# SiLU as one ScalarE activation in a hybrid DeltaNet/GLA layer: `Silu` in place of `Tanh` and a VectorE product

## The chip, the cores and the metric

The kernel runs on one core of a Trainium2 chip. That core has TensorE (PE in the profile; its weight loads are shown apart as PEld), VectorE (DVE), ScalarE (ACT), GpSimd (POOL) and SyncE (SP, which here only issues transfers). Each engine works through its own instruction list in order and waits on semaphores for what other engines have to deliver. The metric is the device time of one launch in microseconds (us), as the median of several runs. Beside it stands one profiled execution, whose trace gives every instruction's start and length.

## The reference: what is computed

One transformer layer on 1024 tokens of width 1024, in fp32. SiLU, x·sigmoid(x), occurs in three places:

```python
qkv = jax.nn.silu(causal_depthwise_conv(jnp.concatenate([gq, gk_, gv], -1), gdn_conv_w[i]))
q_a = l2norm(to_chunks(cq, GDN_HEADS)) * (GDN_HEAD_DIM ** -0.5)
k_a = l2norm(to_chunks(ck, GDN_HEADS))
o_a = gated_delta_rule_chunked(q_a, k_a, v_a, g, beta)
o_a = rmsnorm(o_a, gdn_norm_g[i]) * jax.nn.silu(gz)        # DeltaNet output gate
...
o_b = rmsnorm(gla_chunked(q_b, k_b, v_b, log_fg), gla_norm_g[i]) * jax.nn.silu(lr)   # GLA output gate
merged = jax.nn.sigmoid(gate_a) * y_a + jax.nn.sigmoid(gate_b) * y_b
x = x + merged @ w_out[i]
x = x + CrossAttn(rmsnorm(x), rmsnorm(mem))                # softmax over 256 memory tokens
x = x + relu(rmsnorm(x) @ w1)**2 @ w2                      # then a final rmsnorm
```

The branch A heads (8 of them, gated DeltaNet) need a triangular inverse per chunk and a scan over chunks; the branch B heads (4, gated linear attention, GLA) need exponentials of cumulated gates and a scan.

## The kernel before, in words

Activations are kept transposed: 128 channels on the partitions, tokens along the free axis in two halves of 512. All large products ("dense" products below) are done in three passes: an fp32 operand is split into a rounded high part and the remainder, `split` (L575 to L578): ScalarE copies the high part (L577), VectorE or GpSimd subtracts for the low part (L578), and `mm3` (L532 to L542) issues high·high (L537), high·low (L539) and low·high (L541). Many of the square products also go through a seven-product scheme of block sums (`wino`, `gla_dense`).

The stages in order: the memory keys and values with the first normalisation (`phase0`), the four GLA heads (`phase_gla`), the DeltaNet heads in four pairs (`phase_gdn`), the merge of the two branches (`phase_merge`), the attention and the MLP. In the head stages the dense products of the next head are put into a queue of generators (`push`), and `fill(n)` takes n matmuls from it at chosen points between the small fp32 matmuls of the scans.

The order of the instructions on each engine is not the order of the program text. The kernel is built twice: on the first pass a planner (`Plan`) records all instructions, gives each a cost (`Op.__init__`), works out the dependences, and simulates the five engines (`forward`); of four rounds it keeps the one that ends first, and the second build pins that order on every engine. TensorE takes, of the matmuls whose inputs are planned ready, the one that stands first in the program. An elementwise sum may be given to VectorE or to GpSimd as the plan finds better. ScalarE evaluates functions from a table that holds a set of functions; a function of another set needs a table load first, which the build inserts (`ACT_TABLE_LOAD` in the trace). The planner knows of that by `o.table`, a number for each function's set, and books `LOAD = 1283` ns when it changes.

Where SiLU is computed before the change, with th = tanh(x/2) and the VectorE product (th + 1)·x, which is twice silu(x):

- `push_gla_r` (L976): the GLA output gate r, 16 tiles of 128x512; tanh at L983, product at L984. One tile in four reads its input straight from PSUM.
- `push_conv` (L1193): the convolution for k, q and v of each DeltaNet head, 24 blocks of two halves: first tap on ScalarE (L1209), three more taps on VectorE (L1212, L1215), tanh at L1220 into a tile `tg`, product at L1221.
- `push_gdn_z` (L1421): the DeltaNet output gate z, 16 tiles from PSUM; tanh at L1430, product at L1431.

The factor 2 is taken back in constants: halved gains `ghalf` (L672), 4·EPS in the L2 norms (L1260, L1296) and 0.5 in the scale of v (L1268).

Two other steps are spoken of later. `gdn_subst` inverts the diagonal 32x32 blocks of a pair of heads by 31 steps of products and sums (L1319, L1321), transposes the result on VectorE (L1323, L1325) and copies it into the tiles `PF` (ScalarE, L1331) and `PT` (VectorE, L1332); `gdn_inverse` then begins with the matmuls of L1345 on `PF`. In `gdn_scan` a chunk's chain is z (VectorE, L1387), a matmul (L1394), `dl` (ScalarE, L1396), and the matmuls of L1401 and L1411. `gdn_decay` computes three exponentials per head on ScalarE (L1235, L1239, L1240); the sigmoid gates are tanh with no product (`push_gate`, L1471; `push_gate_pair`, L1000).

Of the kernel before, what the change touches and what calls it, by code (L numbers as in the profile page):

```python
# [18 lines left out]
P = 128  # L19
# [29 lines left out]
def c3(t):  # L49

    return t.rearrange("p (c t) -> p c t", t=P)
# [24 lines left out]
class Op:  # L76
# [6 lines left out]
    def __init__(self, ins, flex):  # L83
        eng = self.eng = ENGINES[ins.engine]
        ins_, outs = [[x for x in q if getattr(x, "bass_ap", None) is not None] for q in (ins.ins, ins.outs)]
        n = size(outs[0])
        psum = lambda x: x.bass_ap.tensor.name[:3] in ("pd_", "ps_")
        self.name, self.opcode, self.acc = ins.name, ins.opcode, []
        for w, q in enumerate((ins_, outs)):
            for x in q:  # L90
                p = x.ap[0][0]
                lows, span = [x.bass_ap.offset % p if p > 1 else x.bass_ap.offset], 0
                for st, k in sorted(x.ap[1:]):
                    if st <= span + 1 or k * len(lows) > 16:
                        span += st * (k - 1)
                    else:
                        lows = [lo + st * i for lo in lows for i in range(k)]
                for lo in lows:
                    self.acc.append((x.bass_ap.tensor.name,) + ((0, HALF) if psum(x) else (lo, lo + span)) + (w,))
        sums = ins.opcode == "TensorTensor"  # L100
        two = sum(size(x) > 1 and not psum(x) for x in ins_) > 1
        self.flex = flex and sums and two and n > 16
        scalar = n > 1 and any(size(x) == 1 for x in ins_)
        far = [x for x in ins_ + outs if not psum(x) and x.ap[-1][0] * 4 > 64]

        scan = 118 * (getattr(ins, "is_tensor_tensor_scan", None) or False)
        times = {"vector": (150 + scan + n * 1.042 + 60 * scalar, 85, 34, 35), "gpsimd": (290 + n * 1.98 if sums else 160 + n * 0.9, 45, 60, 35)}
        if sums and n <= 16:
            times["gpsimd"] = 430 + n * 152, 45, 60, 35
        if ins.opcode == "TensorReduce":  # L110
            times["vector"] = 420, 85, 34, 35
        if ins.opcode == "StreamTranspose":
            times["vector"] = 1880 if far else 1245, 85, 34, 35
        if ins.opcode == "Memset" and far:
            times["gpsimd"] = 450, 45, 60, 35
        self.times = {e: (d - early, early + own, early + lat) for e, (d, early, own, lat) in times.items()}
        if ins.opcode == "DMACopy":
            self.dma, self.cost, self.own, self.lat = True, 60, LAND, LAND
            self.bytes = n * 4 * outs[0].ap[0][1]
        elif eng == "tensor":  # L120
            m = size(ins_[0])
            if ins.is_transpose:
                self.cost = m * 0.85
            elif ins_[0].dtype == F32R:
                self.cost = m * 0.4463 + (4 if m < HALF else 0)
            elif max(m, size(ins_[1])) == 64:
                self.cost = 80
            else:
                self.cost = max(m, size(ins_[1])) * 1.667 + 8
            self.own, self.lat = 0, 203  # L130
        elif eng == "scalar":
            d = (150 if psum(ins_[0]) else 190) + n * 0.84 + 90 * scalar + n * 0.9 * bool(far)
            broken = any(len(x.ap) > 2 and any(st != x.ap[-1][0] * x.ap[-1][1] for st, _ in x.ap[-2:-1]) for x in ins_ + outs)
            self.cost, self.own, self.lat = d - 100 + 240 * (len(outs) > 1) + 140 * broken, 130, 135
            self.table = {AF.Ln: 1, AF.Exp: 2, AF.Tanh: 2}.get(ins.func, 0)
        else:
            self.port = eng == "gpsimd" or (n > 16 or two) and not any(psum(x) for x in ins_ + outs)
            self.take(eng)
# [23 lines left out]
class Plan:  # L162
# [141 lines left out]
    def forward(self, deps, prio):  # L304
# [11 lines left out]
        engs = ("vector", "scalar", "gpsimd", "sync", "tensor")  # L316
        now_q = {e: [] for e in engs + ("flex",)}
        wait_q = {e: [] for e in engs + ("flex",)}
        free = dict.fromkeys(engs + ("port", "ring", "table"), 0.0)
        order = {e: [] for e in engs}  # L320
        events = [0.0]

# [17 lines left out]
        def run(i, t):  # L340
            o = ops[i]
            if o.port:
                t = max(t, free["port"])
                free["port"] = t + o.cost
            if o.table:

                t += LOAD * (o.table != free["table"])
                free["table"] = o.table
            start[i], e = t, t + o.cost
            if o.eng == "tensor":  # L350

                k = int(t / WINDOW)
                if k and work[k - 1] < 0.4 * WINDOW:
                    e += o.cost
                work[k] += e - t
            free[o.eng] = e
            order[o.eng].append(i)
            heapq.heappush(events, e)
            if o.dma:
                e = free["ring"] = max(e, free["ring"]) + o.bytes / RATE  # L360
            done(users[i], e, i)
            done(after[i], t, None)
# [111 lines left out]
class Layer:  # L474
# [180 lines left out]
    def consts(self):  # L655
        nc, a = self.nc, self.a
        cp = self.cp = self.pool(self.ctx, "const", "left")
        self.ident = self.til(cp, [P, P], "ident")
        make_identity(self.tc.nc, self.ident)
        self.mhalf = self.til(cp, [P, 16], "mhalf")  # L660
        nc.vector.memset(self.mhalf, -0.5)
        self.ones = self.til(cp, [P, 1], "ones")
        nc.vector.memset(self.ones, 1.0)
        cols = self.til(cp, [P, 56], "cols")
        nc.scalar.dma_start(cols, a["cols"])
        self.g_mix, self.g_x = cols[:, 0:8], cols[:, 8:16]
        self.g_mem, self.g_mlp = cols[:, 16:24], cols[:, 24:32]
        self.b_gate, self.g_fin = cols[:, 32:36], cols[:, 48:56]
        self.a_log, self.dt_bias = cols[:, 39:40], cols[:, 40:41]

        gh = self.til(cp, [P, 3], "ghalf")
        nc.vector.tensor_scalar(gh, cols[:, 36:39], 0.5, None, MUL)  # L672
        self.g_gdn, self.g_gla = gh[:, 0:1], gh[:, 1:3]
        self.convw = self.til(cp, [P, 24, 4], "convw")
        nc.sync.dma_start(self.convw, a["convw"])
        self.tm = self.til(cp, [P, NB, 2, GH], "tm")
        self.geg = self.til(cp, [P, NB, GH], "geg")
        self.gneg = self.til(cp, [P, NB, GH], "gneg")
# [297 lines left out]
    def push_gla_r(self, sp, h, after=None):  # L976

        nc = self.nc
        sr = [self.dxt(sp) for _ in range(2)]

        def done(j, half, o, x):
            th = self.til(self.tp, [P, HALF], "th", bufs=THB)
            nc.scalar.activation(th, x, AF.Tanh, scale=0.5)  # L983
            nc.vector.scalar_tensor_tensor(o, th, 1.0, x, ADD, MUL)  # L984

        self.push(f"r{h}", self.gla_dense([self.joined(lambda j, half: sr[j][:, half * HALF:(half + 1) * HALF], done)],
                                          after))
        return sr
# [204 lines left out]
    def push_conv(self, wp, sp, sq, name, blk, src, out):  # L1193
# [3 lines left out]
        def gen():  # L1197
# [18 lines left out]
            o = out(acc)  # L1216
            for g in range(2):
                gs = slice(4 * g, 4 * g + 4)
                th = self.til(sq, [P, HALF], "tg", bufs=2)
                nc.scalar.activation(th, acc[:, g * HALF:(g + 1) * HALF], AF.Tanh, scale=0.5)  # L1220
                nc.vector.scalar_tensor_tensor(o[:, gs], c3(th), 1.0, c3(acc)[:, gs], ADD, MUL)  # L1221

        self.push(name, gen())

# [23 lines left out]
    def gdn_keys(self, sp, sq, h, st):  # L1248
# [8 lines left out]
            self.sumsq(sq, pt, ss[:, gs])  # L1257
            nc.vector.tensor_tensor(kd[:, gs, :], c3(pt), bcol(st["kf"][:, gs], P), MUL)
        v = self.til(sq, [P, NB], "vv", bufs=2)
        nc.vector.tensor_scalar(v, ss, 1.0, 4 * EPS, MUL, ADD)  # L1260
        r = self.rsqrt(sq, v, NB)
        b = st["b"] = self.til(sq, [P, NB], "b", bufs=2)
        nb = self.til(sq, [P, NB], "nb", bufs=2)
# [1 line left out]
        nc.vector.tensor_tensor(b, r, r, MUL)  # L1265
        nc.vector.tensor_tensor(b, b, self.tm[:, :, 1, h], MUL)
        nc.vector.tensor_scalar(nb, b, -1.0, None, MUL)
        nc.vector.scalar_tensor_tensor(vs, v, 0.5, r, MUL, MUL)  # L1268
        NT = st["NT"] = self.til(sp, [P, NB, P], "NT", bufs=4)
        for g in range(2):  # L1270
            pt = self.pss()
# [8 lines left out]
    def gdn_queries(self, sp, sq, st):  # L1280
# [12 lines left out]
            pt = self.transpose4([q[:, 4 * g + i, :] for i in range(4)])  # L1293
            self.sumsq(sq, pt, ss[:, 4 * g:4 * g + 4])
        st["eq"] = self.til(sq, [P, NB], "eq", bufs=2)
        nc.vector.tensor_scalar(st["eq"], ss, P * EPS, 4 * EPS * P * EPS, MUL, ADD)  # L1296

    def gdn_subst(self, sp, sq, sts):

# [121 lines left out]
    def push_gdn_z(self, wp, sp, sq, h, st):  # L1421
# [3 lines left out]
        def evict(half, pt):  # L1425
            if half == 0:
                st["sz"] = self.til(sq, [P, 32, 32], "sz", bufs=2).rearrange("p a b -> p (a b)")
            s = slice(half * HALF, (half + 1) * HALF)
            th = self.til(sq, [P, HALF], "tg", bufs=2)
            nc.scalar.activation(th, pt, AF.Tanh, scale=0.5)  # L1430
            nc.vector.scalar_tensor_tensor(st["sz"][:, s], th, 1.0, pt, ADD, MUL)  # L1431

        self.push(f"z{h}", self.g_fm(lambda: self.wunit(wp, self.a["w_gdn"][4 * h + 3]), evict))

# [914 lines left out]
```

## Time and profile before

| | |
|---|---|
| median of 3 runs | 2182.14 us (2181.86 to 2184.06) |
| the profiled execution, own time | 2183.89 us |
| its span in the trace | 2182.2 us |
| PE busy | 2145.7 us, 98% |
| DVE busy | 1589.2 us, 73% |
| ACT busy | 1134.0 us, 52% |
| POOL busy | 177.1 us, 8% |
| granted TensorE clock, mean | 0.995 of full speed |

The trace's times count from the first instruction. The own time of the profiled execution is 1.69 us longer than its span, and 1.75 us above the median of the runs, of which it is not one. "Busy" is the time covered by an engine's instructions; a matmul overlaps the one that follows it, so a busy PE need not be at its peak. A row such as "PE pd L537 <- ACT wop L577: 1.9, 2, 1.3" in a list of waits reads: instructions of line 537 on PE that write a tile pd waited for ScalarE's line 577 writing wop, 1.9 us in total, twice, the longest 1.3 us. In a row of the timeline the first two numbers are the start and the length in us; what stands in brackets is the idle time ahead of it and what ended that.

### The profile page before, as it was taken

How to read it: one execution, taken by the hardware profiler on the slowest of the kernel's cores; microseconds unless marked ns; L12 is line 12 of the kernel's file. 1: busy time of each engine (PE TensorE's matmuls, PEld its weight loads, DVE VectorE, ACT ScalarE, POOL GpSimd, SP SyncE). 2: the span in 40 equal slices, each digit the busy share in tenths (PEclk: the TensorE clock that was granted, in tenths of full speed). 3: DMA queues.
4: the chain of work that ended last, by engine and by line, in shares of the span. 5: the costliest groups of instructions: out<-in, count | busy, mean ns of one | idle time of the engine just before them, and what ended most of it. 6: DMA issues, size and time to landing. Idle time of an engine off the chain costs nothing.

```text
span 2182.2 us, 31863 instructions
## 1 busy us (share of the span) xinstructions
PE 2145.7 (98%) x11504; PEld 1832.7 (84%) x11504; DVE 1589.2 (73%) x2986; ACT 1134.0 (52%) x2295; POOL 177.1 (8%) x221
## 2 busy tenths in 40 slices
PE   8999999999999999999999999999999999999996
PEld 8888978988889888898888888998888888888886
DVE  7845887667696888969779864569967667567746
ACT  7445665355445545465455443565755557444433
POOL 1000000000121322213010000000000000000001
PEclk9999999999999999999999999999999999999998
DMA  7762122121311212111177341336444446688742
GB/s 252 232 226 74 60 102 78 65 80 53 121 39 49 73 40 73 39 49 64 35 262 245 131 154 49 124 115 203 139 150 150 152 158 220 200 269 277 251 138 82
DMA packets 140398, 287.61 MB, mean 132 GB/s; under 512 B 14920, under 2 KB 21448, under 8 KB 140240
## 3 DMA queue, kind: packets, MB, share of 16 engines
q1 hardware_dynamic: 133440, 277.16, 38.0%
q10 hardware_dynamic: 6800, 8.42, 1.1%
q8 instruction: 90, 1.47, 0.3%
q14 instruction: 68, 0.56, 0.1%
HBM read 206.06 MB, written 79.46 MB: 131 GB/s over the span
## 4 chain that ended last, share of the span: by engine, by line
PE 95%; DVE 2%; DMA 1%; issue 1%; ACT 0%; SPq 0%; POOL 0%; DVEq 0%; ACTq 0%; POOLq 0%
PE pd L537 23%; PE pd L541 23%; PE pd L539 22%; PE ps L537 5%; PE ps L541 5%; PE ps L539 5%; PE ps L609 2%; PE ps L1354 1%; PE ps L1345 1%; PE ps L1394 1%; PE ps L1274 1%; PE ps L1411 1%; PE ps L1288 1%; PE ps L1087 1%; PE ps L1401 1%; PE ps L1385 1%
## 5 line engine op out<-in xcount | busy, mean ns | idle before, releaser
L577 ACT ACTIVATE wop<-raw 128x512 fp32r<-128x512 f32 (+1 forms) x472 | 315.3, 672 | 419.7 <-PE pd L541 206.5
L578 DVE TENSOR_TENSOR wop<-raw,wop 128x512 fp32r<-128x512 f32 (+1 forms) x434 | 306.4, 708 | 216.8 <-ACT wop L577 208.9
L541 PE MATMUL pd<-t,wop 128*128 128x512 f32 x300 | 120.3, 401 | 0.0
L537 PE MATMUL pd<-t,wop 128*128 128x512 f32 x300 | 118.1, 394 | 0.0
L1212 DVE SCALAR_TENSOR_TENSOR acc<-pd,convw,acc 128x511 f32<-128x511 f32 x144 | 106.3, 740 | 16.2 <-ACT acc L1209 16.0
L539 PE MATMUL pd<-t,wop 128*128 128x512 f32 x300 | 117.6, 392 | 0.0
L537 PE MATMUL pd<-B1a,wop 128*128 128x512 f32 (+1 forms) x252 | 94.7, 376 | 0.0
L541 PE MATMUL pd<-B1a,wop 128*128 128x512 f32 (+1 forms) x252 | 94.7, 376 | 0.0
L537 PE MATMUL pd<-A1a,wop 128*128 128x512 f32 x180 | 71.0, 394 | 0.0
L539 PE MATMUL pd<-A1a,wop 128*128 128x512 f32 x180 | 70.7, 393 | 0.3 <-DVE A1a L578 0.3
L539 PE MATMUL pd<-B1a,wop 128*128 128x512 f32 (+1 forms) x188 | 69.8, 372 | 0.0
L541 PE MATMUL pd<-A1a,wop 128*128 128x512 f32 x168 | 67.6, 403 | 0.0
L541 PEld LDWEIGHTS pd<-t,wop 128*128 128x128 f32 x300 | 56.4, 188 | 13.2
L539 PEld LDWEIGHTS pd<-t,wop 128*128 128x128 f32 x300 | 56.3, 188 | 13.0
L539 PE MATMUL pd<-B0b,wop 128*128 128x512 f32 x172 | 66.9, 389 | 0.0
L537 PEld LDWEIGHTS pd<-t,wop 128*128 128x128 f32 x300 | 56.4, 188 | 12.1
L1220 ACT ACTIVATE tg<-acc 128x512 f32<-128x512 f32 x48 | 30.0, 630 | 66.8 <-DVE acc L1215 49.5
L578 DVE TENSOR_TENSOR wlo<-raw,wop 128x1024 fp32r<-128x1024 f32 (+1 forms) x37 | 44.9, 1219 | 24.5 <-PE pd L541 14.4
L577 ACT ACTIVATE whi<-raw 128x512 fp32r<-128x512 f32 x70 | 40.9, 624 | 41.2 <-PE pd L539 20.2
L541 PE MATMUL pd<-A0b,wlo 128*128 128x512 f32 x152 | 61.0, 401 | 0.0
L541 PE MATMUL pd<-A1a,wlo 128*128 128x512 f32 x152 | 60.7, 399 | 0.0
L541 PE MATMUL pd<-A0a,wlo 128*128 128x512 f32 x152 | 60.5, 398 | 0.0
(588 smaller groups left out, 6801.9 us busy)
## 6 DMA issues: line engine op xcount, KB each, us to landing
raw<-in_w_dram SPq DMA_DIRECT2D x120, 256.0 KB, 3.6
raw<-in_w_gdn_dram SPq DMA_DIRECT2D x64, 256.0 KB, 2.6
raw<-in_w_dram SPq DMA_DIRECT2D x32, 512.0 KB, 3.7
e<-ad SPq DMA_DIRECT2D x63, 256.0 KB, 4.6
ad<-q SPq DMA_DIRECT2D x45, 256.0 KB, 2.7
rawa<-ad SPq DMA_DIRECT2D x42, 256.0 KB, 4.6
A0b<-tgd SPq DMA_DIRECT2D x32, 256.0 KB, 4.4
ad<-acc SPq DMA_DIRECT2D x30, 256.0 KB, 2.3
```

The source lines that it names most:

```text
L537: nc.tensor.matmul(out, lh, rh, start=first and i == 0, stop=False, skip_group_check=True)
L539: nc.tensor.matmul(out, lh, rl, start=False, stop=False, skip_group_check=True)
L541: nc.tensor.matmul(out, ll, rh, start=False, stop=last and i == n - 1, skip_group_check=True)
L577: nc.scalar.activation(hi, raw, AF.Copy)
L578: (lo_eng or nc.gpsimd).tensor_tensor(lo, raw, hi.bitcast(F32), SUB)
L609: self.nc.tensor.transpose(pt[:, i * P:(i + 1) * P], s, self.ident)
L1087: nc.tensor.matmul(po[:, :256], AT[:, c, :], v[:, c, :], start=True, stop=(c == 0))
L1212: nc.vector.scalar_tensor_tensor(x, pt[:, 0:HALF - d], tap, x, MUL, ADD)
L1220: nc.scalar.activation(th, acc[:, g * HALF:(g + 1) * HALF], AF.Tanh, scale=0.5)
L1274: nc.tensor.matmul(pt[:, i * P:(i + 1) * P], kc, kc, start=True, stop=True)
L1288: nc.tensor.matmul(pt[:, i * P:(i + 1) * P], k[:, 4 * g + i, :], q[:, 4 * g + i, :], start=True, stop=True)
L1345: nc.tensor.matmul(pt[:, i * 96:(i + 1) * 96], NT[:, u + i, :], PF[:, v + i, 0:96], start=True, stop=True)
```

## The change

SiLU becomes one ScalarE instruction with the function `Silu`, in all three places; the tanh, its buffer and VectorE's product go. The product with one half in the gains, the factors of four in the L2 norms and the 0.5 in the scale of v go with them. `Silu` lies in another table set than `Exp`; the planner is told so by bit masks: `Ln` 1, `Exp` 2, `Silu` 4, and `Tanh` 6, since tanh is in both sets. Its simulation now keeps the sets that the loaded table may be as a mask, and books a load where a function's mask has no bit in common with it.

```diff
-            self.table = {AF.Ln: 1, AF.Exp: 2, AF.Tanh: 2}.get(ins.func, 0)
+            self.table = {AF.Ln: 1, AF.Exp: 2, AF.Tanh: 6, AF.Silu: 4}.get(ins.func, 0)
...
-                t += LOAD * (o.table != free["table"])
-                free["table"] = o.table
+                both = o.table & free["table"]
+                t += LOAD * (not both)
+                free["table"] = both or o.table
...
-        gh = self.til(cp, [P, 3], "ghalf")
-        nc.vector.tensor_scalar(gh, cols[:, 36:39], 0.5, None, MUL)
-        self.g_gdn, self.g_gla = gh[:, 0:1], gh[:, 1:3]
+        self.g_gdn, self.g_gla = cols[:, 36:37], cols[:, 37:39]
...   push_gla_r
-            th = self.til(self.tp, [P, HALF], "th", bufs=THB)
-            nc.scalar.activation(th, x, AF.Tanh, scale=0.5)
-            nc.vector.scalar_tensor_tensor(o, th, 1.0, x, ADD, MUL)
+            nc.scalar.activation(o, x, AF.Silu)
...   push_conv
-                th = self.til(sq, [P, HALF], "tg", bufs=2)
-                nc.scalar.activation(th, acc[:, g * HALF:(g + 1) * HALF], AF.Tanh, scale=0.5)
-                nc.vector.scalar_tensor_tensor(o[:, gs], c3(th), 1.0, c3(acc)[:, gs], ADD, MUL)
+                nc.scalar.activation(o[:, gs], c3(acc)[:, gs], AF.Silu)
...   gdn_keys, gdn_queries
-        nc.vector.tensor_scalar(v, ss, 1.0, 4 * EPS, MUL, ADD)
+        nc.vector.tensor_scalar(v, ss, 1.0, EPS, MUL, ADD)
-        nc.vector.scalar_tensor_tensor(vs, v, 0.5, r, MUL, MUL)
+        nc.vector.tensor_tensor(vs, v, r, MUL)
-        nc.vector.tensor_scalar(st["eq"], ss, P * EPS, 4 * EPS * P * EPS, MUL, ADD)
+        nc.vector.tensor_scalar(st["eq"], ss, P * EPS, EPS * P * EPS, MUL, ADD)
...   push_gdn_z
-            th = self.til(sq, [P, HALF], "tg", bufs=2)
-            nc.scalar.activation(th, pt, AF.Tanh, scale=0.5)
-            nc.vector.scalar_tensor_tensor(st["sz"][:, s], th, 1.0, pt, ADD, MUL)
+            nc.scalar.activation(st["sz"][:, s], pt, AF.Silu)
```

More of the change, by code (lines that the diff above doesn't have):

```diff
@@ L318, in forward @@
         wait_q = {e: [] for e in engs + ("flex",)}
-        free = dict.fromkeys(engs + ("port", "ring", "table"), 0.0)
+        free = dict.fromkeys(engs + ("port", "ring"), 0.0)
+        free["table"] = 0
         order = {e: [] for e in engs}
```

## The prediction

> **What bounds the kernel now.** I read the page's first and fourth parts, then the busy times by stage, then who TensorE waited for. Page, engines and chain of waits:
>
> ```profile
> span 2182.2 us, 31863 instructions
> PE 2145.7 (98%) x11504; PEld 1832.7 (84%) x11504; DVE 1589.2 (73%) x2986; ACT 1134.0 (52%) x2295; POOL 177.1 (8%) x221
> ...
> PE 95%; DVE 2%; DMA 1%; issue 1%; ACT 0%; SPq 0%; POOL 0%; DVEq 0%; ACTq 0%; POOLq 0%
> ```
>
> Busy time by stage (GLA heads, DeltaNet heads); columns are the stretch, its length, then PE, PEld, DVE, ACT, POOL, each with its count, granted clock, DMA share, GB/s:
>
> ```profile
> 205.00:558.00 353.00, 353.00 (x2042) 302.64 (x2041) 257.86 (x412) 194.16 (x322) 19.62 (x21) 1.00 0.21 69
> 558.00:1122.00 564.00, 559.13 (x3320) 486.30 (x3318) 450.67 (x1084) 290.55 (x833) 128.60 (x169) 1.00 0.20 68
> ```
>
> In these two stages, which hold all SiLU, PE is idle 0.0 and 4.87 us; ScalarE is busy 55% and 52% of them, VectorE 73% and 80%. Who PE waited for, over the whole span:
>
> ```profile
> PE ps L620 <- DVE acc L646: 7.4, 3, 5.5
> PE pd L537 <- ACT mT L692: 5.5, 2, 5.2
> PE pd L541 <- DVE wlo L578: 3.0, 4, 1.5
> PE ps L1345 <- issue: 2.8, 3, 0.9
> PE pd L537 <- ACT wop L577: 1.9, 2, 1.3
> PE pd L537 <- ACT gst L757: 1.0, 1, 1.0
> PE pd L537 <- ACT whi L577: 0.9, 1, 0.9
> ```
>
> By their lines the first three and L757 belong to the first stage or to column sums of norms, which the change does not touch. What the change can reach is L1345 (2.8), one wait of 1.3 for `wop` where the merge begins, and 0.9 for `whi` where the DeltaNet stage begins: 5.0 us, 0.23% of the time. So this is a kernel bound by TensorE, and the question is less what the change saves than whether it brings a wait to an engine that has nearly none.
>
> **The change part by part.** *VectorE products.* The three rows are lines 984, 1221 and 1431 over the whole span; the fourth is L1221 in the second pair of heads, the fifth all engines in a stretch of that pair:
>
> ```profile
> 0.00:2182.20 2182.20, 10.94 (x16) 1.00 0.39 132
> 0.00:2182.20 2182.20, 34.53 (x48) 1.00 0.39 132
> 0.00:2182.20 2182.20, 10.83 (x16) 1.00 0.39 132
> 660.00:796.00 136.00, 8.78 (x12) 1.00 0.17 56
> 700.00:800.00 100.00, 99.06 (x553) 85.29 (x552) 89.59 (x214) 53.28 (x157) 27.47 (x37) 1.00 0.17 55
> ```
>
> 10.94 + 34.53 + 10.83 = 56.3 us of VectorE go, 80 instructions; `ghalf` and the constants are too small to count. PE waited for none of the three, so on the path this is worth 0. Indirectly it brings the triangular inverse forward, since VectorE is 90% busy there (fifth row): see L1345.
>
> *ScalarE, the function.* Lines 1220 and 1430:
>
> ```profile
> L1220 ACT ACTIVATE tg<-acc 128x512 f32<-128x512 f32 x48 | 30.0, 630 | 66.8 <-DVE acc L1215 49.5 <-DVE acc L1212 11.7 <-DVE b L1265 2.4
> ...
> L1430 ACT ACTIVATE tg<-pd 128x512 f32<-128x512 f32 x16 | 9.4, 586 | 19.3 <-PE pd L541 19.3
> ```
>
> The same number of ScalarE instructions on the same shapes stays. No row shows Silu. I bound one from below by the 586 ns of the cheapest tanh, and from above by two tanh, 1260 ns; I take 630, since shape and engine are those of L1220. At the upper end 80 x 0.63 = 50 us more on an engine with 159 + 273 us free in the two stages: 0 on the path at both ends so long as no chain waits on it. The chain of a block gets shorter by a product (0.7 us).
>
> *Table loads.* In the order of the changed kernel there are 35 loads where the order of before has 11: 7 more among the GLA heads, 16 in the DeltaNet stage where there were none, and 1 ahead of the first softmax exponential. What a switch costs stands in ScalarE's timeline at 361 us:
>
> ```profile
> 361.13 0.62 ACT L577 ACTIVATE wop<-raw 128x512 fp32r<-128x512 f32 x1
> 361.65 0.63 ACT L1000 ACTIVATE dx<-dx 128x512 f32<-128x512 f32 x1
> 362.29 1.28 ACT L846 ACT_TABLE_LOAD   x1
> 363.59 1.06 ACT L846 ACTIVATE ex<-ex 128x1024 f32<-128x1024 f32 x1
> ```
>
> Without a switch, L1000 starts 0.52 us after L577 (they overlap by 0.1). With one, L846 starts 1.94 after L1000: a switch costs 1.42 us. 24 x 1.42 = 34 us of ScalarE; the DeltaNet stage goes from 52% to 56%. The planner books 1.28 of the 1.42, so its order leaves ScalarE 0.14 late. That reaches PE only where a matmul is placed just as ScalarE ends: in the scans, where `dl` (L1396) feeds L1401 and L1411. In the changed order these matmuls stand behind a few more dense ones at two steps of each of the first three scans, which covers the booked load. Unbooked: 6 x 0.14 = 0.8 us at most, 0 at least. I take 0.4, in the middle, since the rows do not show how near each is.
>
> The Trainium skill (ScalarE: Activation LUTs, What ACT_TABLE_LOAD costs) gives 1283 ns for the load and about 1380 ns for a drain, 2.66 us for every switch. The trace agrees on the load and not on the drain: 361.65 + 0.63 = 362.28, the load starts at 362.29, and the next activation 0.02 after its end.
>
> The softmax load executes while ScalarE has nothing else to do there; were it exposed, 1.42 us once, but the wait list has no PE wait after the merge begins.
>
> *L1345.* In the second pair, transposes on VectorE, copies on ScalarE, then PE (rows of three engines' timelines):
>
> ```profile
> 790.70 2.04 DVE L1325 STREAM_TRANSPOSE X<-Pm 128x1024 f32<-128x1024 f32 x1
> 792.78 3.33 ACT L1331 ACTIVATE PF<-X 32x512 f32<-32x512 f32 x3 [4.38 <-DVE X L1325]
> 796.20 0.99 PE L1345 MATMUL ps<-PF,NT 128*128 128x96 f32 x7 [0.94 <-issue]
> ```
>
> PE is held until the last `PF` copy ends (796.11), 0.94 us later than the plan put it. The transpose, the copies and the matmul all stay, so I expect this lateness to stay: three pairs, 2.8 us, change 0. The changed order puts L1345 18 dense matmuls earlier in the second to fourth pair, 18 x 0.23 = 4.1 us (the step between dense matmuls, 1120.26 to 1120.49 in the next fence); the 12 products gone from a pair (8.78 us, row above) on a VectorE 90% busy are more than that. The ends: all 2.8 us go, or the inverse comes no earlier and each wait grows by 4.1.
>
> *Start of the merge.* Timelines of SyncE, ScalarE and PE, and how long these four transfers took to land:
>
> ```profile
> 1113.39 2.93 SPq L506 DMA_DIRECT2D raw<-in_w_bgla_dram  x4
> 1120.96 0.60 ACT L1471 ACTIVATE acc<-pd 128x512 f32<-128x512 f32 x1 [0.69 <-PE pd L541]
> 1121.53 0.63 ACT L577 ACTIVATE wop<-raw 128x512 fp32r<-128x512 f32 x1
> 1120.26 0.39 PE L539 MATMUL pd<-A1a,whi 128*128 128x512 f32 x1
> 1120.49 0.39 PE L541 MATMUL pd<-A1a,wlo 128*128 128x512 f32 x1
> 1122.21 0.50 PE L537 MATMUL pd<-B0a,wop 128*128 128x512 f32 x1 [1.34 <-ACT wop L577]
> DMA to landing us min/median/max: 8.1/8.7/9.4
> ```
>
> ScalarE has the last gate's tanh ahead of the first `wop`, and that tanh needs the last matmul of the stage. In the changed order `wop` stands ahead of it. It then hangs on its weights alone: issued at 1113.39, landed 8.1 later, at 1121.5, too late by themselves. But they too are issued earlier: the last pair's output transposes stand 15 dense matmuls (3.4 us) earlier, and with them the stores that stand before these loads in SyncE's queue. One row of gate store still bounds the loads; I take 2 us earlier, so `wop` is done at 1120.2 and the wait of 1.34 goes. Ends: -1.34 and 0.
>
> *Start of the DeltaNet stage.* `whi` waits for a weight transfer at 561 us; nothing in its chain is edited: 0, ends -0.9 and +0.9.
>
> *More switches between small and dense matmuls.* The changed order has 8 more. PE's timeline:
>
> ```profile
> 1070.91 0.69 PE L1394 MATMUL ps<-v,NT 128*128 128x128 f32 x4
> 1071.36 0.48 PE L537 MATMUL pd<-A0b,whi 128*128 128x512 f32 x1
> 1071.67 0.40 PE L539 MATMUL pd<-A0b,whi 128*128 128x512 f32 x1
> ```
>
> The dense matmul behind small ones takes 0.31 to the next start, others 0.23 (at the merge, above): 8 x 0.08 = 0.7 at most. I take 0.2, as the small ones overlap it.
>
> Elsewhere PE's order is unchanged: its instructions are the same in kind and number, and in the same sequence up to the first pair of heads and again from soon after the merge's start to the end.
>
> Sum: -1.3 + 0.4 + 0.2 = -0.7 us. Against the profiled execution's own 2183.89 that is 2183.2; that execution lay 1.75 above the median of the runs, so against the median 2182.14 - 0.7 = 2181.4.
>
> **The rivals.** *The inverse comes late* (slower). The plan counts on VectorE's relief to bring L1345 4.1 us forward. If the gain is lost, as the steps of the inverse are handed out anew between VectorE and GpSimd, PE stands up to 4.1 more in each of three pairs: 2181.4 + 12.3 = 2193.7. It decides (over 0.2%, 4.4 us, about what a measurement of this kernel can tell from no change) from 1.7 us per pair on, when less than 2.4 of the 4.1 come. For it: the wait of 0.94 in three pairs shows the plan too early on this very chain. Against: 8.78 us of relief per pair.
>
> *A switch costs twice its load* (slower). If ScalarE drained at a switch of sets for another 1.28 us that the plan does not book, the six steps at which `dl` follows a load would be late by 6 x 1.28 = 7.7: 2189.1. Against: the timeline above, with 0.02 us after the load. This is the page's rule cited above.
>
> *All reachable waits go* (faster). A lighter VectorE could end the L1345 waits and the one for `whi` also: 2182.14 - 5.0 + 0.6 = 2177.7 at the end of it. For it: the inverse gets relief. Against: the wait follows the plan's idea of the chain, not the load.
>
> *The change does not do what it says.* Were Silu as long as two tanh, ScalarE would rise by 50 us and the blocks' chain would be no shorter; with the cover above, 2182 to 2184, no change.
>
> *VectorE sets the pace*, and its 56.3 us show: 2126. The wait lists have no PE wait for it in these stages; 0.
>
> **How the numbers follow.** The forecast, within 2178.5 to 2184.5, has 0.68; Silu slower than tanh 0.06 (no change either); all waits gone 0.11, of which 0.09 ends below 2177.8; the late inverse 0.10 and the dear switch 0.05, both above 2186.5. Faster 0.09, same 0.68 + 0.06 + 0.02 = 0.76, slower 0.15. The range from 2177.5 to 2187.5 takes in the forecast, most of the faster case and the milder half of the late inverse.
>
> **What would show it.** Right: DVE near 1533 us busy, ACT near 1165 us with 35 loads of 1.28, PE busy within 2 us of now, no `wop` wait at the merge, three L1345 waits near 0.9. Wrong: an L1345 wait of 2 us or more; PE waits at L1401, L1411 or L1394; an activation that starts more than 0.1 us after its load without waiting for data; Silu rows off 630 ns by more than a tenth; a new PE wait for `wop` after the merge begins, where the transfers of operands are issued in a new order.

## The result, and the profile after

The changed kernel takes 2186.11 us in the median of 20 runs, the kernel before 2183.32 in 20 runs beside it: ratio 1.0015, 95% interval [1.0008, 1.0021]. It is 0.15% slower, about 3 us. 2181.4 was forecast; the time lies within the range given, on the other side of the kernel before.

The page of the changed kernel, its first and fourth parts:

```profile
span 2184.6 us, 31782 instructions
PE 2153.0 (99%) x11504; PEld 1832.7 (84%) x11504; DVE 1542.4 (71%) x2916; ACT 1168.0 (53%) x2319; POOL 167.0 (8%) x210
...
PE 92%; DVE 3%; DMA 3%; ACT 1%; issue 1%; SPq 0%; POOL 0%; DVEq 0%; ACTq 0%; POOLq 0%
```

VectorE is busy 46.8 us less (1533 us were forecast; it is 1542.4, and GpSimd, which shares the sums with it, 10.1 us less than before) and ScalarE 34.0 us more (1165 forecast). PE, whose 11504 matmuls are the same in number, is busy 7.3 us longer. Who PE waited for, the head of the list (lines of the matmuls in `mm3` are two higher than before, L1341 stands for the old L1345):

```profile
PE ps L622 <- DVE acc L648: 7.2, 3, 5.5
PE pd L539 <- ACT mT L692: 5.5, 1, 5.5
PE pd L539 <- ACT A1b L579: 1.0, 1, 1.0
PE pd L539 <- ACT gst L757: 0.9, 1, 0.9
PE pd L539 <- ACT whi L579: 0.9, 1, 0.9
PE pd L543 <- DVE wlo L580: 0.9, 2, 0.5
PE pd L539 <- ACT wop L579: 0.8, 2, 0.6
PE ps L636 <- DVE rs_o L574: 0.8, 2, 0.4
PE ps L1397 <- ACT dl L1392: 0.5, 1, 0.5
```

The three waits of the inverse (2.8 us) and the wait of 1.3 at the start of the merge are not there. So PE waits less and the kernel is slower: the loss lies in how fast PE works. Busy time by stage, columns as in the prediction; first the changed kernel (GLA, DeltaNet, the stretch from the merge on), then the last stretch of the kernel before:

```profile
205.00:558.00 353.00, 353.00 (x2036) 301.61 (x2036) 250.32 (x400) 199.58 (x328) 16.22 (x19) 1.00 0.21 70
558.00:1122.00 564.00, 562.08 (x3330) 488.42 (x3328) 416.23 (x1039) 317.80 (x854) 117.14 (x158) 1.00 0.21 71
1122.00:2140.00 1018.00, 1017.71 (x4861) 849.62 (x4860) 703.26 (x1176) 526.32 (x935) 16.00 (x12) 1.00 0.53 173
```

```profile
1122.00:2140.00 1018.00, 1017.79 (x4891) 855.26 (x4892) 707.92 (x1189) 527.75 (x941) 11.79 (x9) 1.00 0.52 175
```

Read the counts: in 1018 us of which PE is idle 0.3 us or less in both, 4861 matmuls fit after and 4891 before. Thirty matmuls at 0.23 us are 6.9 us, lost in a stretch that holds no SiLU and in which the change edits nothing; the granted clock is 1.00 in both. When the starts of the matmuls of the two traces are laid side by side, the changed kernel is 5.5 us ahead just behind the start of the merge (2.2 of them were there at 205 us already, behind the first stage, in which the change drops `ghalf` alone). It loses that lead bit by bit, some 0.4 us in every 50 us, save in stretches that stream B tiles almost alone (1271 to 1372 us of the kernel before), and from 2118 us on it is 2.3 us behind.

The same 132 dense matmuls, which stream an A or t tile one after another near the end, show it. PE's timeline, the first of them and the one behind the last, before and then after:

```profile
1870.76 0.40 PE L537 MATMUL pd<-A1a,wop 128*128 128x512 f32 x1
...
1900.99 0.40 PE L537 MATMUL ps<-B0a,wop 128*128 128x512 f32 x1
```

```profile
1870.43 0.40 PE L539 MATMUL pd<-A1a,wop 128*128 128x512 f32 x1
...
1901.24 0.40 PE L539 MATMUL ps<-B0a,wop 128*128 128x512 f32 x1
```

30.23 us before, that is 229.0 ns from one start to the next; 30.81 us after, 233.4 ns. The length of a row (0.40) does not show it, since the ends of matmuls are modelled: only the distance of starts does. By kind of tile over the whole stretch, a matmul that streams A or t goes from 229.2 to 233.4 ns, and one that streams a B tile stays at 227.3 and 227.2.

What did the change do to the A and t tiles? It dropped `ghalf`. These 12 bytes took 32 bytes of each partition in the pool of constants, on the left side of SBUF, and every tile allocated on that side behind it now lies 32 bytes lower: in the two builds A1a is at byte 35648 of its partitions, not 35680. The weights `wop` and the B tiles are allocated from the right side and stay where they were.

### The profile page after: what moved, and what is told of

It reads as the page before. It is cut to its first block, busy times and chain, and to the rows that moved or that the text cites. A ratio compares the mean times of both kernels' runs of the same rounds, so it can differ in the third digit from the quotient of the medians.

```text
span 2184.6 us, 31782 instructions
## 1 busy us (share of the span) xinstructions
PE 2153.0 (99%) x11504; PEld 1832.7 (84%) x11504; DVE 1542.4 (71%) x2916; ACT 1168.0 (53%) x2319; POOL 167.0 (8%) x210
## 4 chain that ended last, share of the span: by engine, by line
PE 92%; DVE 3%; DMA 3%; ACT 1%; issue 1%; SPq 0%; POOL 0%; DVEq 0%; ACTq 0%; POOLq 0%
PE pd L543 22%; PE pd L539 22%; PE pd L541 22%; PE ps L539 5%; PE ps L543 5%; PE ps L541 5%; PE ps L611 2%; PE ps L1350 1%; PE ps L1270 1%; PE ps L1284 1%; PE ps L1390 1%; PE ps L1341 1%; PE ps L1407 1%; PE ps L1085 1%; DMA raw<-in_w_dram 1%; PE ps L1397 1%
## 5 line engine op out<-in xcount | busy, mean ns | idle before, releaser
L543 PE MATMUL pd<-A1b,wlo 128*128 128x512 f32 x152 | 59.7, 393 | 0.0
```

Of the source, the lines that this page charges most:

```text
L543: nc.tensor.matmul(out, ll, rh, start=False, stop=last and i == n - 1, skip_group_check=True)
```

## Experiments

Two theories at the start. **Addresses**: the step of a dense matmul depends on where the streamed tile lies, and the loss has nothing to do with SiLU. **The change itself**: denser work, table loads or a re-ordered stage slow PE later, by the clock or by contention. The edit for addresses is one unused tile in the pool of constants. In the kernels of e1 to e7, e10 and e11 each engine's instructions stand in the order of the kernel that they start from.

**e1: the 32 bytes put back.**

```
         self.g_gdn, self.g_gla = cols[:, 36:37], cols[:, 37:39]
+        self.til(cp, [P, 8], "space")
```

> The changed kernel with an unused 32-byte tile where ghalf stood, so that every tile above it in the left half of SBUF lies at its address of before; the order of the instructions on all engines is that of the changed kernel. Theory A (without ghalf the left tiles lie 32 bytes lower, and matmuls that stream from them step more slowly): the dense step with moving operand A1a, A1b, t in the merge, attention and MLP goes back from 233-234 to 226-232 ns, 7 us less in the span than the changed kernel, and the rest of the change then shows a gain: about 0.998 of the kernel before. Theory B (the change itself slows the late stages, by its new order of transfers or by a lower clock): 1.0015 as the changed kernel.

2179.75 us, ratio 0.9984 [0.9976, 0.9993]. The 132 matmuls take 30.23 us again.

**e2: the kernel before, less the 32 bytes** (the halved gains go into unused columns of `cols`).

```
-        gh = self.til(cp, [P, 3], "ghalf")
+        gh = cols[:, 41:44]
```

> The kernel before with ghalf written into three unused columns of cols instead of a tile of its own: the left tiles lie 32 bytes lower, as in the changed kernel, and nothing else differs. Theory A: the same matmuls step at 233-234 ns, about 7 us longer than before, ratio 1.0033. Theory B: 1.000.

2190.70 us, 1.0039 [1.0026, 1.0052]; the 132 matmuls take 30.80 us. Addresses are confirmed from both sides, and the change itself is cleared: with addresses equal it is faster by 0.16% (e1 against before). The last stretch in e1 and in e2:

```profile
1122.00:2140.00 1018.00, 1016.48 (x4885) 853.34 (x4884) 706.68 (x1183) 528.95 (x939) 16.05 (x12) 1.00 0.53 172
```

```profile
1122.00:2140.00 1018.00, 1018.00 (x4864) 850.37 (x4865) 704.19 (x1180) 526.59 (x938) 11.69 (x9) 1.00 0.53 174
```

4885 with the SiLU change and the old addresses, 4864 without the SiLU change and with the new addresses.

**e3 and e4: other places.** As e1 with 64 and with 224 bytes in place of 32.

> The changed kernel with an unused tile of 64 bytes: the left tiles lie 32 bytes higher than before the change, at the same residue of 64 as in the changed kernel. Theory A, if the residue of 64 decides: as the changed kernel, 1.0015. Theory A with a longer period: another value, between 0.996 and 1.003. Theory B: 1.0015.

> The changed kernel with an unused tile of 224 bytes: the left tiles have the residue of 256 (32) that the tiles B0a to B1b have, whose matmuls step at 226.7 ns before and after. Theory A, if the residue of 256 decides: all dense steps of the late stages at about 227, some 10 us less than the changed kernel, 0.997 or less of the kernel before. Theory A, if the residue of 64 decides: as the first kernel of this call, about 0.998. Theory B: 1.0015.

e3: 2188.64 us, 1.0025 [1.0016, 1.0034]. e4: 2169.94 us, 0.9943 [0.9931, 0.9955], faster than both kernels. The 132 matmuls and the last stretch of e4:

```profile
1862.10 0.39 PE L539 MATMUL pd<-A1a,wop 128*128 128x512 f32 x1
...
1892.02 0.39 PE L539 MATMUL ps<-B0a,wop 128*128 128x512 f32 x1
...
1122.00:2140.00 1018.00, 1015.54 (x4907) 858.24 (x4906) 708.97 (x1187) 528.22 (x941) 15.88 (x12) 1.00 0.53 172
```

29.92 us, 226.7 ns a step, where the kernel before has 229.0. In e1 and e4 the A tiles lie at the same place modulo 64 (35680 and 35872 are both 32 above a multiple), and the times differ by 0.4%: what repeats has a longer period than 64 bytes.

**e5: the kernel before at the places of e4.** Behind `ghalf`:

```
+        self.til(cp, [P, 48], "space")
```

> The kernel before with an unused tile of 192 bytes per partition behind the column constants, so that all tiles of the left side lie where the fastest version so far has them (A1a at 35872, 32 above a multiple of 256); every engine's order of instructions is that of before. If addresses and the SiLU change add up, this is the kernel before less what the 192 bytes gave the changed kernel (2169.94 against 2179.75, 9.8 us): 2182.9 - 9.8 = 2173.1, ratio 0.9955, and the SiLU change is worth 3.2 us here too. If the SiLU change is what makes the good addresses pay, this stays above 2178. Steps between dense matmuls from 1130 us on: 226.5 to 227.5 ns on all three lines in the first case.

2173.78 us, 0.9958 [0.9945, 0.9970]: 192 unused bytes alone speed up the kernel before by 0.42%. At these places the SiLU kernel has 0.9943, so SiLU is worth 0.15% here too: the two effects add.

**e6 and e7: the place of the streamed tile, or its distance from the weights?** A pool on the right side is opened before all others, which moves weights and B tiles down:

```
         cp = self.cp = self.pool(self.ctx, "const", "left")
+        self.til(self.pool(self.ctx, "top", "right"), [P, 48], "space2")    # e6, with e1's 32 bytes on the left
+        self.til(self.pool(self.ctx, "top", "right"), [P, 16], "space2")    # e7, with e4's 224 bytes on the left
```

> The changed kernel with 32 unused bytes on the left side (A1a at 35680, 96 above a multiple of 256, as before) and 192 on the right, so that the weights (wop) and the B tiles lie 192 lower: weights 32, B tiles 96 above a multiple of 256. The distances between all streamed tiles and weights are those of the fastest version, 64 bytes further up. Order of instructions as in the changed kernel. If the distance between the streamed tile and the weights sets the step: as the fastest version, 2170 +- 1.5, steps of 226.5 to 227.5 ns for A and B tiles from 1130 us on and 229 in the GLA stage. If the streamed tile's own place sets it: A tiles at 227 to 232 as with the 32 bytes alone, B tiles no longer at 226.7 but like A, time 2180 or above, GLA 232 to 233.

> The changed kernel with 224 unused bytes on the left side (A1a at 35872, 32 above a multiple of 256, as in the fastest version) and 64 on the right: weights at 160, B tiles at 224 above a multiple of 256. Order of instructions as in the changed kernel. If the streamed tile's own place sets the step: A tiles at 226.5 to 227.5 ns, GLA stage at 229, B tiles slower than 226.7; time 2170 plus what B loses, up to 2175. If the distance to the weights sets it (A to weights is 128 here, as it is in the kernel before): A tiles at 227 to 232, B tiles (64 to weights, unchanged) at 226.7, time 2175 to 2181.

Two addresses are mixed up in these texts: the ring of weights at 212960 (224 above a multiple of 256) serves the GLA stage, that of the late stages begins at 122144 (32 above). So A lies 64 from the late weights before, and 64 in e7. What was to be told apart is not touched, as e6 keeps all distances of e4, and e7 those of the kernel before.

e6: 2171.06 us, 0.9944 [0.9932, 0.9957], 226.7 ns in the 132 matmuls, with the A tiles where they are in the kernel before. e7: 2181.16 us (0.16 above the range expected for the distance), 0.9988 [0.9979, 0.9997], 229.0 ns, with the A tiles where e4 has them. It is the distance; the place of the tile alone is refuted twice.

**e10 and e11: the distance in the GLA stage.** As e4, and only the first ring of weights moves:

```
+            self.til(self.pool(ctx, "pad", "right"), [P, 48], "space2")    # e11: [P, 32]
             self.wp = self.pool(ctx, "w1", "right")
```

> The fastest version so far (224 unused bytes on the left) with 192 unused bytes above the ring of weights of the first stages, so that these weights (212768, ring of the normalisation and GLA stages) too lie 32 above a multiple of 256, like the streamed A and t tiles. Streamed tile and weights then are a multiple of 256 bytes apart in all dense stages. Order of instructions as in the changed kernel. If the step is set by that distance and is shortest at 0: the GLA stage goes from 229.2 to 226.7 ns, 353 us / 229 ns = 1540 matmuls x 2.5 ns = 3.9 us, time 2166 +- 1.5, ratio 0.9925. If each ring of weights has its own best distance: 229 to 234 ns there, time 2169 to 2176.

> As the run with 192 bytes above the first ring, but 128: these weights lie 96 above a multiple of 256 and the streamed tiles 192 (or -64) from them; GLA stage alone changed against 224 bytes on the left. If the step depends on the size of the distance and not on its sign: as at +64, 229.2 ns, 2170. If 192 is one more of the slow ones: 231 to 235 ns, 2173 to 2179.

e10: 2170.46 us, 0.9945 [0.9931, 0.9958]; e11: 2175.14 us, 0.9964 [0.9952, 0.9977]. The GLA step went to 227.0 in e10 as expected, and the time did not follow. The GLA stage has also matmuls of 256 columns that stream the weights and keep t or A tiles as stationary operand, and for these the order is turned round: 115.5 ns in e4, 120.0 in e10. 667 x 4.5 = 3.0 us lost stand against 850 x 2.3 = 2.0 us won. In e11 the distance is 192, that is -64, and the step 233.3: the sign counts, since at +64 it is 229.2. The fastest times of this study, 2169.94, 2171.06 and 2170.46 (e4, e6, e10), cannot be told apart.

Put together, the mean step between dense matmuls of 512 columns that stream A or t tiles (some 850 of them in the GLA stage and 1550 behind the merge in each trace), against the distance, that is the streamed tile's address less the weights', modulo 256:

| kernels | late: distance, ns | GLA: distance, ns |
|---|---|---|
| before, e1, e7 | 64: 229.2 to 229.5 | 128: 232.7 to 232.8 |
| after, e2 | 32: 233.4 | 96: 233.4 |
| e3 | 96: 233.6 | 160: 234.2 |
| e4, e5, e6 | 0: 226.8 to 226.9 | 64: 229.2 to 229.3 |
| e10 | 0: 226.9 | 0: 227.0 |
| e11 | 0: 226.8 | 192: 233.3 |

One reading fits both stages: 0 costs 227, 64 costs 229, every other distance tried 233 to 234. (The distances of before and e7 differ by 256 bytes, and their steps are the same.) The DeltaNet stage fits as well: there activations and weights are both on the left side, at distance 0 in every kernel, and its step is 227.7 to 228.0 in all of them.

**e8 and e9: why did the waits of the inverse go?** Both as e1, at the addresses of before. In e8 the convolution's Silu writes `tg`, and VectorE copies it with an operation of the old product's form; in e9 the output gate z does the same too.

```
-                nc.scalar.activation(o[:, gs], c3(acc)[:, gs], AF.Silu)
+                th = self.til(sq, [P, HALF], "tg", bufs=2)
+                nc.scalar.activation(th, acc[:, g * HALF:(g + 1) * HALF], AF.Silu)
+                nc.vector.scalar_tensor_tensor(o[:, gs], c3(th), 1.0, c3(th), MUL, ALU.max)
```

> The changed kernel with the 32 unused bytes, in which the convolution's Silu writes the tile tg and VectorE copies it to its place with an operation of the product's form and shape (48 x 0.72 us): ScalarE as in the changed kernel, VectorE relieved of 22 us only instead of 56. If the waits at the first matmul of the inverse went because VectorE was relieved: two to three of them come back at 0.7 to 1.0 us, and the time is that of the 32 bytes alone (2179.75) plus 2 to 3.5 us, 2182 to 2183. If they went for another reason (the order on ScalarE, an earlier start of the chain's matmuls): none comes back, 2179 to 2181.

> As the run before it with the convolution's copies (the changed kernel, 32 unused bytes), and the DeltaNet output gate's Silu too writes a tile that VectorE copies to its place with an operation of the product's shape: VectorE keeps 64 of the 80 operations in all, at 45 of 56 us; ScalarE as in the changed kernel. The plan puts the first matmul of the inverse where it stands in the kernel before. If VectorE's products ahead of the inverse made the waits there (four gate products of 0.68 us in a pair are 2.7 us, which is the 0.9 of the wait and the 1.8 us by which the plan brought the matmul forward without them): three waits of 0.7 to 1.0 us are back, time 2.0 to 3.5 us above that of the convolution's copies alone (ratio to before 0.9995 against 0.9982). If ScalarE's shorter path or the table did it: no wait, ratio 0.998.

e8: 2178.59 us, 0.9982 [0.9973, 0.9990]; e9: 2179.93 us, 0.9986 [0.9978, 0.9995]. None of the three waits came back in either, against what the theory of VectorE's products expected. Both kernels also have another order on every engine and 37 table loads, not 35; and in e9 the merge's wait for `wop` is back (1.3 us), with the gate's tanh ahead of `wop` on ScalarE again. ScalarE's copies into `PF` and the first matmul of the inverse, second pair, in e1, e8 and e9:

```profile
781.04 4.65 ACT L1328 ACTIVATE PF<-X 32x512 f32<-32x512 f32 x4 [1.13 <-DVE X L1322]
788.97 3.71 PE L1342 MATMUL ps<-PF,NT 128*128 128x96 f32 x32
```

```profile
789.13 4.64 ACT L1330 ACTIVATE PF<-X 32x512 f32<-32x512 f32 x4 [1.39 <-DVE X L1324]
792.76 1.44 PE L1344 MATMUL ps<-PF,NT 128*128 128x96 f32 x11
```

```profile
791.87 3.41 ACT L1330 ACTIVATE PF<-X 32x512 f32<-32x512 f32 x3 [3.24 <-DVE X L1324]
795.38 1.88 PE L1344 MATMUL ps<-PF,NT 128*128 128x96 f32 x15
```

The matmul reads columns 0 to 95 of `PF`, which the first three of the four copies write. In e1 the third copy ends at 784.57 (the copies stand one by one in the trace) and the matmul starts 4.40 us later: there is slack. In e8 and e9 the matmul starts 0.10 us behind the end of the third copy (in e9 at 795.28), as it does in the kernel before, so the copies still release it; but PE comes from its previous matmul without a gap worth listing, where before it stood for 0.94 us. Against the flow of dense matmuls the copies come earlier by about 0.9 us in e9 (the matmul stands where it stood before), 0.8 + 8 x 0.23 = 2.6 us in e8 (eight places earlier), and 0.94 + 18 x 0.23 + 4.40 = 9.5 us in e1. So the copies come the earlier, the more of VectorE's work is gone, but the first 0.9 us, all that the waits needed, come with the products of convolution and gate still on VectorE. What gives these 0.9 us in e9 (the new order of the steps between VectorE and GpSimd, the sixteen products of r, or the dropped operand) was not tried.

## Why the prediction was wrong

**Where it failed.** The steps "`ghalf` and the constants are too small to count" and "elsewhere PE's order is unchanged". Both hold for VectorE's time and for the order, and neither asks where the tiles go. The missing term: 1550 late matmuls x (233.4 - 229.2) = 6.5 us and 850 in the GLA stage x (233.4 - 232.8) = 0.5 us, together 7.0. Measured: e1 to after, 0.0031 x 2182.9 = 6.8 us. (Matmuls of 256 columns moved too and add little: 640 behind the merge lose 1.0 us in all, the 667 of the GLA stage win 0.5.) No rival had this mechanism; that the time stayed in the range is owed to the rivals on the slow side, none of which occurred.

**The SiLU change by itself** is e1 against before: 0.16% [0.07%, 0.24%], 3.5 us, where the sum gave 0.7. By its terms:

- *L1345, taken at 0.* All three waits went, 2.8 us. Here the prediction's own numbers were against it: 8.78 us of relief less 4.1 us of earlier placement leave 4.7 us, which is more than the 0.94 that was to stay (in e1 the 9.5 measured less 4.1 leave 5.4). It priced the chain and then did not use the price. The rival in which all reachable waits go had this mechanism.
- *Start of the merge, -1.3.* Right, and by the reason given: the transfers are issued earlier and `wop` no longer stands behind the gate's activation. In the changed kernel the issue moved by 5.6 us in the trace's time; PE's lead is 3.6 there, which leaves 2.0 against PE's own flow, just what was taken. The rest of the margin is that the first weights landed 6.6 us behind their issue (1107.76 to 1114.35), not 8.1. That is not certain: in e4 and e11, in the same order, they landed 8.3 and 7.7 us behind it, and PE waited 1.7 and 0.9 us for `wop`. SyncE, ScalarE and PE of the changed kernel:

```profile
1107.76 3.42 SPq L508 DMA_DIRECT2D raw<-in_w_bgla_dram  x4
1114.35 0.63 ACT L579 ACTIVATE wop<-raw 128x512 fp32r<-128x512 f32 x1 [0.77 <-DMA raw<-in_w_bgla_dram]
1117.38 0.60 ACT L1465 ACTIVATE acc<-pd 128x512 f32<-128x512 f32 x1 [2.40 <-PE pd L543]
1117.14 0.39 PE L539 MATMUL pd<-B0a,wop 128*128 128x512 f32 x1
```

- *Table loads, +0.4.* The count is right, 35 loads; the cost on PE is not shown. There is one wait for `dl`, 0.5 us (L1397 in the list above, the old L1401, which the prediction named as a sign of being wrong), but no load holds it up:

```profile
797.90 1.28 ACT L1235 ACT_TABLE_LOAD   x1
806.31 0.21 ACT L1235 ACTIVATE kf<-kf 128x8 f32<-128x8 f32 x1 [7.13 <-DVE kf L1234]
808.53 1.06 ACT L1231 ACTIVATE dm<-dm 128x1024 f32<-128x1024 f32 x1 [2.01 <-DVE dm L1230]
809.50 0.61 ACT L1392 ACTIVATE dl<-ps,b 128x128 f32<-128x128 f32 x2
809.90 0.75 PE L1397 MATMUL ps<-dl,kdt 128*128 128x128 f32 x4 [0.50 <-ACT dl L1392]
```

The load was over at 799.18; `dl` stands behind an exponential that waited 2.0 us for VectorE. e1, in the same order, has no wait for `dl` in its list. That 0.5 is near 0.4 is luck. A switch itself, on ScalarE in the DeltaNet stage, and groups of ScalarE over the span:

```profile
598.00 1.28 ACT L1217 ACT_TABLE_LOAD   x1
599.29 0.63 ACT L1217 ACTIVATE q<-acc 128x512 f32<-128x512 f32 x1
...
L1217 ACT ACT_TABLE_LOAD x8 | 10.3, 1283 | 0.1
L1217 ACT ACTIVATE acc<-acc 128x512 f32<-128x512 f32 x16 | 10.1, 633 | 29.2 <-DVE acc L1213 19.8 <-DVE acc L1210 9.2
L1425 ACT ACTIVATE sz<-pd 128x512 f32<-128x512 f32 x16 | 9.5, 592 | 8.3 <-PE pd L543 8.0
```

The activation starts 0.01 us behind its load. The Trainium skill (ScalarE: Activation LUTs, What ACT_TABLE_LOAD costs) adds a drain of about 1380 ns to every switch; with 24 more switches the trace shows none: behind every load but the first of the kernel the next activation starts within 0.02 us, or it waits for data from VectorE. The rival built on the drain is refuted.

- *Silu as long as tanh* (630 ns): 633 on an SBUF operand and 592 from PSUM, where tanh had 630 and 586. Right.
- *More switches between small and dense matmuls, +0.2*: they are there, 142 in the DeltaNet stage against 134, but no cost shows: in e1 PE gains 1.0 us on the kernel before in each of the second and third pairs, no less than the wait of 0.94 that went.
- *DeltaNet's start, 0*: `whi` waits 0.9, as before.
- *The inverse comes late*: refuted by the 4.40 us of slack.
- *Not foreseen, and small*: in e1 PE also has waits that the kernel before does not have, 0.4 us for a v from VectorE at 1099 us, 0.45 for an A1b from VectorE at 1152, 0.73 for a q from ScalarE at 1539 and 0.3 for an A0b from VectorE at 2013, and it waits 0.25 longer for `whi`. From 205 us on PE's waits, without those of the last stage, fall from 5.1 us in the kernel before to 3.0 in e1, and PE's lead in the two traces grows by as much, from 1.8 to 3.9. The median's 3.5 has an interval from 1.5 to 5.2 that takes this 2.0 in. That -0.7 - 2.8 gives just 3.5 is luck: the 0.4 and 0.2 in it did not show, and the new waits are not in it. Single traces settle no more: e1 and e7, equal in their order and in these distances, lie 2.8 us apart at 195 us, at the end of the first stage.

In short, the forecast of a small gain was right for what the diff is about, too small by the inverse's waits, and turned into a loss by 32 bytes.

## What to carry to other kernels

A tile that goes or comes, however small, moves every tile behind it: compare the addresses of the two builds, above all the distance of streamed tiles from weights, before a change of some tenths of a per cent is put down to its instructions, and put unused bytes in place of a tile that is taken out when the change itself is to be judged. A slower PE without waits is seen in the count of matmuls in equal stretches and in the distances of their starts, not in the busy time or in the length of a row. And where a chain's relief is priced, take the price to the wait at its end: relief minus earlier placement, against the wait.

## What the runs showed of the hardware

The rate of back-to-back fp32r matmuls depends on the distance in SBUF between the tile that is streamed and the weights, modulo 256 bytes: about 227 ns a step at 0, 229 at 64, 233 to 234 at 32, 96, 128, 160 and 192, for 512 columns. At 256 columns with the operands' roles exchanged (GLA stage, the distance again that of the streamed tile from the stationary one) it is 115.5 ns at 192 (e4) and 120.0 at 0 (e10), so that no single distance is best for all shapes. Whether it is the weights of the running matmul or of the next that count can't be told, as all weights of a ring have the same place modulo 256. From the worst to the best arrangement tried, with the same instructions, the whole kernel moves by 0.8% (e3 1.0025 to e4 0.9943, e2 1.0039 to e5 0.9958), five times what the SiLU change is worth. The mechanism was not isolated. The Trainium skill (TensorE: Matmul & The Clock Gate, Step-by-step: what each phase is for) gives TensorE two independent read ports, one for the streamed operand and one for the weights, and says that loading the next weights takes no read bandwidth from the running matmul. At distance 0 no run here speaks against that; at other distances something between the two operands costs up to 7 ns in 227, and whether it is the loading of weights is not shown. Taken as a rule that the two never disturb each other, it does not hold here, and the measurement decides.
